# A position bias read in turned order through GpSimd's queue, and two later forget-bias operations, in a two-layer attention and feed-forward block

## The chip, the cores and the metric

The kernel runs on one core of one Trainium2 chip. The metric is the device time of one execution in microseconds (us); lower is better. The core has five engines with a queue each: PE (matmuls), DVE (elementwise and reductions on VectorE), ACT (ScalarE), POOL (GpSimd) and SP, which here only issues transfers. Each engine works through its own queue in order; semaphores tie the queues together. Transfers between DRAM and the on-chip memory are issued from a queue, too, and land some time after.

## The reference, cut to what matters

Two layers (DEPTH), each a mixer and a gated feed-forward part, for 256 tokens of width 1024, all in f32. The mixer has three kinds of heads: 4 FoX heads with a forget gate, 4 MoBA heads and 8 MLA heads. With 256 tokens and a MoBA block of 256 there is one block, so a MoBA head is causal attention with a T5 bias. The two things that this change touches are the forget bias and the T5 bias:

```python
def dense_causal_attention(q, k, v, log_decay_cum=None):
    ...
        s = jnp.einsum('bhqd,bhkd->bhqk', q_i, k).astype(jnp.float32) * scale
        if log_decay_cum is not None:
            s = s + blk[2][..., None] - log_decay_cum[:, :, None, :]
        qpos = t0 + jnp.arange(Q_BLOCK)
        s = jnp.where(kpos[None, :] <= qpos[:, None], s, -jnp.inf)
        p = jax.nn.softmax(s, axis=-1)
...
def moba_attention(q, k, v, t5_table):
    ...
        dist_own = qp[:, None] - (own * MOBA_BLOCK + offs)[None, :]
        s_own = (jnp.einsum('bhqd,bhkd->bhqk', q_i, k_own).astype(jnp.float32) * scale
                 + table_t[:, t5_bucket(dist_own)])
        s_own = jnp.where(dist_own >= 0, s_own, -jnp.inf)
...
def hybrid_mixer(h, w_in, b_forget, ...):
    ...
    log_f = jax.nn.log_sigmoid((f_logit + b_forget).astype(jnp.float32))
    F = jnp.cumsum(log_f, axis=1).transpose(0, 2, 1)
    o_f = dense_causal_attention(heads(q_f, FOX_HEADS), heads(k_f, FOX_HEADS), heads(v_f, FOX_HEADS), F)
    o_m = moba_attention(heads(q_m, MOBA_HEADS), heads(k_m, MOBA_HEADS), heads(v_m, MOBA_HEADS), t5_table)
```

The T5 bias depends on the distance of query and key and the head alone, and is the same in both layers.

## The kernel before, in words

Weights stream from DRAM through SP's queue. Each matmul weight is split into two float32r halves: ScalarE copies it to `wh` (L102), DVE subtracts for `wl` (L103), and PE makes three matmuls of each product (`mm3`, L146, and `mm3t`, L168). The raw weights have four buffers, the halves six each. A second stream, `adaw`, carries the weights of the modulation; four buffers hold it, and a chunk is either multiplied on PE (`adap`, L274) or reduced on DVE (L266, 128x1024).

Layer 0 begins with a warm-up of PE by 13 matmuls on a tile `zero` that GpSimd makes, then the sum of squares of `x` per token tile: ScalarE squares (L356), DVE adds, GpSimd takes the power (`rs`, L343), DVE makes a diagonal matrix `diag` of it (L361). Then `phase_a` (L578) goes through eight chunks of 128 rows; each multiplies a chunk of `adaw`, turns a chunk of `x` by the diagonals (`xT`, L949), modulates it on ScalarE (`hv`, L367), and adds its part to the products cq, ckv, qf and kf. In the last chunk the table `shp` is loaded. Then follow the norms, the value projections `vps`, the MLA pairs (`mla_pair`, L749), the FoX pairs and the MoBA pairs (`head_pair`, L769 on), between them further projections `qkp` and steps of the modulation (`fill`); then the output projection `y` and the feed-forward part, which makes up most of the time. Layer 1 repeats this with other stages at its start.

The T5 bias (`t5_bias`, L226) was computed behind the value projections of layer 0. A table `tab` and a one-hot matrix `oneh` are loaded; DVE repeats the table (`trep`), four matmuls give the band of 384 distances for each head on 32 partitions (`tp`, L235), ScalarE evicts it (`band`, L238), and four transfers write it to a DRAM tensor `scr`, so that it stands there 128 times per head (L242). One transfer then reads `mobab` from it, with each partition shifted by one element (L245). The MoBA softmax adds `mobab` (L433 and L435).

For the forget gate, `gqs` are the summed gates by token; `rows_of` (L299) transposes them, writes `row` to DRAM (`rowsgk`, L306) and reads it back onto all partitions (`gk`, L309). `fox_bias` (L725) makes `fb` of one head from `gk`, `gqs` and the mask in two operations of DVE: 128x128 (L729) and 128x256 (L732).

The order within each engine's queue comes from a scheduler that sorts by the program's order, by priorities and by its own estimates of time; `order_after` adds an order between two instructions without a wait. In `fox_bias` L729 was bound to come after the last maximum of a softmax so far (`last["max"]`, L435), L732 wasn't. Transfers on SP's queue are issued in that queue's order: a transfer that waits holds all behind it.

Of the kernel before, what the change touches and what calls it, by code (L numbers as in the profile page):

```python
# [8 lines left out]
F32 = mybir.dt.float32  # L9
# [4 lines left out]
P = 128  # L14
# [30 lines left out]
def block_kernel(ctx, tc, A, out):  # L45
# [141 lines left out]
    shp = const.tile([P, 896], F32, name="shp")  # L187
# [38 lines left out]
    def t5_bias():  # L226
        tab = wk.tile([P, 4], F32, tag="tab", bufs=1, name="tab")
        SP.dma_start(tab, A["t5"])
        oneh = wk.tile([P, 384], F32, tag="e", bufs=4, name="oneh")
        SP.dma_start(oneh, A["k_onehot"])  # L230
        trep = wk.tile([P, 4, 32], F32, tag="kt", bufs=2, name="trep")
        DVE.tensor_copy(trep, tab[:, :, None].to_broadcast([P, 4, 32]))
        tp = pg("tp")
        for hd in range(4):
            PE.matmul(tp[32 * hd:32 * hd + 32, :384], trep[:, hd, :], oneh, start=True, stop=True,  # L235
                      tile_position=(0, 32 * hd))
        band = wk.tile([P, 384], F32, tag="e", bufs=4, name="band")
        ACT.activation(band, tp[:, :384], AF.Copy)  # L238

        scr = dram.tile([4, 4, 32, 384], F32, name="scr")  # L240
        for q in range(4):
            SP.dma_start(scr[:, q, :, :], band)  # L242
        base = scr[:, :, :, :]
        toep = bass.AP(base.tensor, base.offset + 127, [[383, P], [P * 384, 4], [1, S]])
        SP.dma_start(mobab, toep)  # L245
# [276 lines left out]
    def mixer(l, h, prepare, fill, after):  # L522
# [168 lines left out]
        if l == 0:  # L691
            for i, ps in enumerate(rest):
                qk_out(ps, i)
            w1.extend(value_weights(l))
            for t in range(2):
                value1(t)
            t5_bias()
# [27 lines left out]
        def fox_bias(hd):  # L725
# [3 lines left out]
            i = DVE.scalar_tensor_tensor(fb[:, 0:P], gk[:, 0:P], gqs[:, 2 * hd:2 * hd + 1], mask[:, P:S],  # L729
                                         op0=ALU.subtract, op1=ALU.add)  # L730
            order_after(i, last["max"])
            DVE.scalar_tensor_tensor(fb[:, P:384], gk, gqs[:, 2 * hd + 1:2 * hd + 2], mask,  # L732
                                     op0=ALU.subtract, op1=ALU.add)
# [262 lines left out]
def _constants():  # L996
# [6 lines left out]
    out["k_ones"] = np.ones((P, P), f)  # L1003
    out["k_mask"] = np.where(j[None, :] <= P + p[:, None], 0.0, NEG).astype(f)
# [11 lines left out]
    oneh = np.zeros((P, 384), f)  # L1016
# [100 lines left out]
```

## Time and profile before

| | |
|---|---|
| median of 3 runs | 676.29 us (673.01 to 677.72) |
| the profiled execution | 677.55 us, of which the span from first to last instruction is 675.7 us |
| busy: PE, DVE, ACT, POOL | 638.3, 451.2, 365.7, 52.8 us |
| mean granted clock of TensorE | 0.986 of full |
| moved | 155.29 MB, mean 230 GB/s |

PE is busy for 94% of the span, so idle time of PE and stretches at the lower of its two clock levels are what there is to read; the slices of the page show where they are, the waits name who was waited for, and the chain of waits follows back what ended last. Times in rows are us from the span's start unless marked ns. In a chain row the first number is the start, the second the duration; in a timeline row the bracket at the end gives the idle time before and what ended it.

### The profile page before, as it was taken

The page shows a single profiled execution, that of the slowest core. Times are in us where ns is not written, and L with a number is a line of the kernel's source. Part 1 is how long each engine was busy: PE and PEld are TensorE (multiplying, and loading weights), DVE is VectorE, ACT ScalarE, POOL GpSimd, SP SyncE. Part 2 cuts the span into 40 slices and gives each one's busy share as a digit, 9 for nine tenths or more (in the row PEclk, how much of TensorE's full clock was granted, in tenths as well). Part 3 has the DMA queues.
Part 4 walks back from the last instruction along what each step waited for, and adds up shares of the span by engine and source line. Part 5 has one row for each costly group of instructions (what it writes and reads, how often), then busy time and mean ns, then how long its engine had stood idle before and what let it go on. Part 6 is the DMA issues. An engine that isn't in the chain of part 4 may idle for free.

```text
span 675.7 us, 12112 instructions
## 1 busy us (share of the span) xinstructions
PE 638.3 (94%) x4543; PEld 564.7 (84%) x4543; DVE 451.2 (67%) x969; ACT 365.7 (54%) x758; POOL 52.8 (8%) x90
## 2 busy tenths in 40 slices
PE   7988769999999999999998999899899999999996
PEld 5877658567999999999978988768799999999994
DVE  2557277878867777797658864875878755555543
ACT  4348436868644444443467764886764444444431
POOL 1000011431000000000001011250100000000000
PEclk8999979999999999999999999999999999999999
DMA  8968586786478898898845865651568676565511
GB/s 311 407 214 287 161 315 221 266 289 214 123 255 308 288 357 307 312 325 287 303 157 173 270 229 185 219 189 64 187 196 271 223 237 182 183 185 183 185 60 63
DMA packets 44410, 155.29 MB, mean 230 GB/s; under 512 B 5136, under 2 KB 6464, under 8 KB 44352
## 3 DMA queue, kind: packets, MB, share of 16 engines
q1 hardware_dynamic: 44352, 154.52, 67.7%
q8 instruction: 36, 0.59, 0.4%
q14 instruction: 22, 0.18, 0.1%
HBM read 152.64 MB, written 1.86 MB: 229 GB/s over the span
## 4 chain that ended last, share of the span: by engine, by line
PE 76%; DVE 8%; DMA 6%; ACT 3%; POOL 3%; issue 2%; SPq 0%; DVEq 0%; POOLq 0%; ACTq 0%
PE gu L148 11%; PE gu L149 11%; PE gu L150 11%; PE y L172 8%; PE y L170 8%; PE y L171 8%; DMA adaw<-in_w_ada_dram 4%; DVE wl L103 3%; PE adap L274 2%; PE o L478 2%; DMA scr<-band 2%; POOL rs L343 1%; PE qkp L150 1%; PE s L460 1%; PE qkp L148 1%
## 5 line engine op out<-in xcount | busy, mean ns | idle before, releaser
L103 DVE TENSOR_TENSOR wl<-raw_gu,wh 128x1024 fp32r<-128x1024 f32 (+1 forms) x100 | 108.5, 1095 | 67.8 <-ACT wh L102 66.8
L102 ACT ACTIVATE wh<-raw_gu 128x1024 fp32r<-128x1024 f32 (+1 forms) x100 | 94.2, 956 | 92.0 <-PE gu L149 62.5
L148 PE MATMUL gu<-h0fL,wh 128*128 128x256 f32 x304 | 86.2, 283 | 0.0
L148 PE MATMUL gu<-h1fL,wh 128*128 128x256 f32 x304 | 86.2, 283 | 0.0
L149 PE MATMUL gu<-h0fH,wh 128*128 128x256 f32 x304 | 86.0, 283 | 0.0
L149 PE MATMUL gu<-h1fH,wh 128*128 128x256 f32 x304 | 86.0, 283 | 0.0
L150 PE MATMUL gu<-h0fH,wl 128*128 128x256 f32 x304 | 86.0, 283 | 0.0
L150 PE MATMUL gu<-h1fH,wl 128*128 128x256 f32 x304 | 86.0, 283 | 0.0
L266 DVE CUSTOM_DVE_ANT_0 adaw<-adaw,crow 128x1024 f32<-128x1024 f32 x64 | 77.9, 1227 | 11.8 <-DMA adaw<-in_w_ada_dram 11.7
L102 ACT ACTIVATE wh<-raw_dn 128x1024 fp32r<-128x1024 f32 x44 | 46.6, 1060 | 54.8 <-issue 33.3
L171 PE MATMUL y<-wh,hid 128*128 128x512 f32 x176 | 69.6, 396 | 0.0
L170 PE MATMUL y<-wh,hid 128*128 128x512 f32 x176 | 69.5, 396 | 0.0
L172 PE MATMUL y<-wl,hid 128*128 128x512 f32 x176 | 69.5, 395 | 0.0
L103 DVE TENSOR_TENSOR wl<-raw_dn,wh 128x1024 fp32r<-128x1024 f32 x44 | 53.6, 1223 | 21.8 <-ACT wh L102 21.7
L149 PEld LDWEIGHTS gu<-h1fH,wh 128*128 128x128 f32 x304 | 58.3, 192 | 0.4
L149 PEld LDWEIGHTS gu<-h0fH,wh 128*128 128x128 f32 x304 | 58.3, 192 | 0.4
L148 PEld LDWEIGHTS gu<-h1fL,wh 128*128 128x128 f32 x304 | 58.2, 192 | 0.4
L148 PEld LDWEIGHTS gu<-h0fL,wh 128*128 128x128 f32 x304 | 58.2, 192 | 0.4
L150 PEld LDWEIGHTS gu<-h1fH,wl 128*128 128x128 f32 x304 | 58.3, 192 | 0.0
L150 PEld LDWEIGHTS gu<-h0fH,wl 128*128 128x128 f32 x304 | 58.3, 192 | 0.0
L343 POOL TENSOR_TENSOR rs<-rs,mhalf 128x1 f32<-128x1 f32 x16 | 11.0, 688 | 439.4 <-DVE rs L342 439.4
L172 PEld LDWEIGHTS y<-wl,hid 128*128 128x128 f32 x176 | 33.0, 188 | 8.0
(331 smaller groups left out, 1482.2 us busy)
## 6 DMA issues: line engine op xcount, KB each, us to landing
adaw<-in_w_ada_dram SPq DMA_DIRECT2D x96, 512.0 KB
raw_gu<-in_w_gu_dram SPq DMA_DIRECT2D x88, 512.0 KB
raw_dn<-in_w_dn_dram SPq DMA_DIRECT2D x44, 512.0 KB
raw_out<-in_w_out_dram SPq DMA_DIRECT2D x16, 512.0 KB
raw_b<-in_w_b_dram SPq DMA_DIRECT2D x12, 512.0 KB
raw_a<-in_w_a_dram SPq DMA_DIRECT2D x8, 448.0 KB
raw_uq<-in_w_uq_dram SPq DMA_DIRECT2D x4, 512.0 KB
raw_vm<-in_w_vm_dram SPq DMA_DIRECT2D x4, 512.0 KB
```

Of the source, the lines that this page charges most:

```text
L102: ACT.activation(dst_h, src, AF.Copy)
L103: return DVE.tensor_tensor(dst_l, src, dst_h.bitcast(F32), op=ALU.subtract)
L148: chain(PE.matmul(ps, w[0], x[1], start=start, stop=False))
L149: chain(PE.matmul(ps, w[0], x[0], start=False, stop=False))
L150: chain(PE.matmul(ps, w[1], x[0], start=False, stop=stop))
L170: PE.matmul(ps, x[1], w[0], start=start, stop=False)
L171: PE.matmul(ps, x[0], w[0], start=False, stop=False)
L172: PE.matmul(ps, x[0], w[1], start=False, stop=stop)
L266: i = DVE.tensor_tensor_reduce(out=raws[u], in0=raws[u], in1=crow, op0=ALU.mult, op1=ALU.add, scale=1.0, scalar=0.0, accum_out=sb[:, u:u + 1])
L274: chain(PE.matmul(ps[32 * g:32 * g + 32, :], crep[:, kc, :], raws[kc // 4][:, g * 256:(g + 1) * 256], start=kc < 4, stop=kc >= 4, tile_pos ...
L343: POOL.tensor_tensor(r, r, mhalf, op=ALU.pow)
L478: PE.matmul(o[64 * u:64 * u + 64, lo:lo + P], v[:, u * 64:(u + 1) * 64], ps[u][:, i * P:(i + 1) * P], start=start, stop=stop, tile_positio ...
```

## The change

It has two parts. The T5 bias is prepared at the very start: table and one-hot matrix have 64 rows instead of 128, one matmul makes the band on 4 partitions, one transfer writes the 6 KB of it to DRAM, and two transfers (two heads each) read from it rows that are shifted the other way round, so that partition p holds what partition 127-p needs; all of these are issued from GpSimd's queue. In the first layer two matmuls by a turned identity `flip`, a new part of `shp`, put the rows in their order, and ScalarE evicts them into `mobab`. In `fox_bias` both operations are now bound to come after the last maximum.

```diff
-    shp = const.tile([P, 896], F32, name="shp")
+    shp = const.tile([P, 1024], F32, name="shp")
+    flip = shp[:, 896:1024]
...
-    def t5_bias():
-        tab = wk.tile([P, 4], F32, tag="tab", bufs=1, name="tab")
-        SP.dma_start(tab, A["t5"])
-        oneh = wk.tile([P, 384], F32, tag="e", bufs=4, name="oneh")
-        SP.dma_start(oneh, A["k_onehot"])
-        trep = wk.tile([P, 4, 32], F32, tag="kt", bufs=2, name="trep")
-        DVE.tensor_copy(trep, tab[:, :, None].to_broadcast([P, 4, 32]))
+    def t5_load():
+
+        tab = wk.tile([64, 4], F32, tag="tab", bufs=1, name="tab")
+        POOL.dma_start(tab, A["t5"])
+        oneh = wk.tile([64, 384], F32, tag="e", bufs=4, name="oneh")
+        POOL.dma_start(oneh, A["k_onehot"])
         tp = pg("tp")
-        for hd in range(4):
-            PE.matmul(tp[32 * hd:32 * hd + 32, :384], trep[:, hd, :], oneh, start=True, stop=True,
-                      tile_position=(0, 32 * hd))
-        band = wk.tile([P, 384], F32, tag="e", bufs=4, name="band")
-        ACT.activation(band, tp[:, :384], AF.Copy)
-
-        scr = dram.tile([4, 4, 32, 384], F32, name="scr")
-        for q in range(4):
-            SP.dma_start(scr[:, q, :, :], band)
-        base = scr[:, :, :, :]
-        toep = bass.AP(base.tensor, base.offset + 127, [[383, P], [P * 384, 4], [1, S]])
-        SP.dma_start(mobab, toep)
+        PE.matmul(tp[0:4, :384], tab, oneh, start=True, stop=True)
+        band = wk.tile([4, 384], F32, tag="e", bufs=4, name="band")
+        ACT.activation(band, tp[0:4, :384], AF.Copy)
+        scr = dram.tile([4, 384], F32, name="scr")
+        POOL.dma_start(scr, band)
+        base = scr[:, :]
+        turned = [wk.tile([P, 512], F32, tag="yg", bufs=2, name="t5rows") for _ in range(2)]
+        for n in range(2):
+            POOL.dma_start(turned[n], bass.AP(base.tensor, base.offset + n * 768, [[1, P], [384, 2], [1, S]]))
+        return turned
+
+    def t5_bias(turned):
+        for n in range(2):
+            ps = pg("t5b")
+            PE.matmul(ps, flip, turned[n], start=True, stop=True)
+            ACT.activation(mobab[:, 2 * n:2 * n + 2, :], ps.rearrange("p (h j) -> p h j", h=2), AF.Copy)
+
+    t5 = t5_load()
...
-            i = DVE.scalar_tensor_tensor(fb[:, 0:P], gk[:, 0:P], gqs[:, 2 * hd:2 * hd + 1], mask[:, P:S],
-                                         op0=ALU.subtract, op1=ALU.add)
-            order_after(i, last["max"])
-            DVE.scalar_tensor_tensor(fb[:, P:384], gk, gqs[:, 2 * hd + 1:2 * hd + 2], mask,
-                                     op0=ALU.subtract, op1=ALU.add)
+            for t, sl, m in ((0, slice(0, P), mask[:, P:S]), (1, slice(P, 384), mask)):
+                i = DVE.scalar_tensor_tensor(fb[:, sl], gk[:, :sl.stop - sl.start],
+                                             gqs[:, 2 * hd + t:2 * hd + t + 1], m, op0=ALU.subtract, op1=ALU.add)
+                order_after(i, last["max"])
...
+    out["k_flip"] = np.eye(P, dtype=f)[::-1].copy()
...
-    oneh = np.zeros((P, 384), f)
+    oneh = np.zeros((64, 384), f)
```

The call of `t5_bias` stays behind the value projections in the program's order. The changed instructions stand in the queues as follows; the rows are line (of the kernel before or of the changed one), operation, tiles written and read, shape.

SP's queue from the weights `raw_b` of layer 0 on, first before, then changed:

```order
L126 DMA raw_b<-in_w_b_dram 128x1024 x4
L126 DMA raw_out<-in_w_out_dram 128x1024
L242 DMA scr<-band 4x32x384 x4
L306 DMA rowsgk<-row 8x128
L126 DMA raw_out<-in_w_out_dram 128x1024
L245 DMA mobab<-scr 128x4x256
L309 DMA gk<-rowsgk 128x1024
L257 DMA adaw<-in_w_ada_dram 128x1024 x3
L126 DMA raw_out<-in_w_out_dram 128x1024 x2
```

```order
L126 DMA raw_b<-in_w_b_dram 128x1024 x4
L126 DMA raw_out<-in_w_out_dram 128x1024
L263 DMA adaw<-in_w_ada_dram 128x1024
L312 DMA rowsgk<-row 8x128
L126 DMA raw_out<-in_w_out_dram 128x1024
L263 DMA adaw<-in_w_ada_dram 128x1024
L315 DMA gk<-rowsgk 128x1024
L126 DMA raw_out<-in_w_out_dram 128x1024
L263 DMA adaw<-in_w_ada_dram 128x1024 x2
L126 DMA raw_out<-in_w_out_dram 128x1024
```

The four writes of `scr` and the read of `mobab` are gone from between `raw_out` and `gk`, and `adaw` loads stand earlier.

DVE's queue from the reciprocals of the first MLA pair's softmax (`ri`) to the second pair's `qx`, `nm` and `ri`, first before, then changed (ISA is a reduction: of `adaw`, or of scores with a maximum):

```order
L443 RECIPROCAL ri<-sm 128x2 x2
L732 SCALAR_TENSOR_TENSOR fb<-gk,gqs,shp 128x256
L103 TENSOR_TENSOR wl<-raw_b,wh 128x1024
L763 TENSOR_TENSOR qx<-qp,qt 128x512
L266 ISA adaw,adasum<-adaw,crow 128x1024
L266 ISA adasum 128x1
L266 ISA adaw,adasum<-adaw,crow 128x1024
L266 ISA adasum 128x1
L320 TENSOR_TENSOR gcol<-adasum,first 128x2
L433 ISA e,mx<-s,shp 128x128
```

```order
L272 ISA adaw,adasum<-adaw,crow 128x1024
L272 ISA adasum 128x1
L449 RECIPROCAL ri<-sm 128x2 x2
L326 TENSOR_TENSOR gcol<-adasum,first 128x2
L327 TENSOR_TENSOR gcol<-gcol,first 128x2
L103 TENSOR_TENSOR wl<-raw_b,wh 128x1024
L768 TENSOR_TENSOR qx<-qp,qt 128x512
L272 ISA adaw,adasum<-adaw,crow 128x1024
L272 ISA adasum 128x1
L439 ISA e,mx<-s,shp 128x128
L439 ISA mx 128x1
```

The `fb` that needs `gk` no longer stands ahead of the split of raw_b and of `qx`; one `adaw` reduction moved ahead of the reciprocals.

POOL's queue at the start, from the small constants on, first before, then changed (`rs` is the power for one of the two token tiles):

```order
L192 MEMSET mhalf 128x1
L194 MEMSET zf 128x128
L198 MEMSET epsc 128x1
L196 CAST zero<-zf 128x128
L343 ISA
L343 TENSOR_TENSOR rs_132<-rs_132,mhalf 128x1
L343 TENSOR_TENSOR rs_142<-rs_142,mhalf 128x1
```

```order
L193 MEMSET mhalf 128x1
L195 MEMSET zf 128x128
L199 MEMSET epsc 128x1
L230 DMA tab<-in_t_dram 64x4
L197 CAST zero<-zf 128x128
L232 DMA oneh<-in_k_onehot_dram 64x384
L349 ISA
L349 TENSOR_TENSOR rs_146<-rs_146,mhalf 128x1
L238 DMA scr<-band 4x384
L349 TENSOR_TENSOR rs_156<-rs_156,mhalf 128x1
L242 DMA t5rows<-scr 128x2x256 x2
```

Two loads stand among the constants, and the write of `scr`, which waits for `band`, stands between the powers of the two token tiles.

## Rows read from the trace of the kernel before

**Rows 1.** The page's part 2: busy tenths of PE and granted clock by slice

```profile
PE   7988769999999999999998999899899999999996
...
PEclk8999979999999999999999999999999999999999
```

**Rows 2.** PE's waits, 0 to 135 us: total us, times, longest

```profile
PE s L458 <- DVE qx L763: 8.1, 2, 7.2
...
PE pt L451 <- POOL e L445: 1.7, 2, 1.2
```

**Rows 3.** DVE's waits, 40 to 135 us

```profile
DVE fb L732 <- DMA gk<-rowsgk: 8.3, 1, 8.3
```

**Rows 4.** The chain of waits, 58 to 112 us

```profile
69.29 10.34 DMA scr<-band
...
80.12 5.44 DMA gk<-rowsgk
...
85.99 1.22 DVE wl L103
...
87.86 1.22 PE s L458 x4
...
90.79 1.47 PE o L478 x10
...
92.78 0.21 PE qkp L148
...
94.18 0.12 PE qkp L149
...
103.97 5.04 DMA adaw<-in_w_ada_dram
```

**Rows 5.** The timeline of SP's queue, 62 to 112 us

```profile
67.42 3.10 SPq L242 DMA_DIRECT2D scr<-band  x4
71.03 0.86 SPq L306 DMA_DIRECT2D rowsgk<-row  x1
```

**Rows 6.** The timeline of all engines, 74 to 114 us

```profile
76.91 0.48 POOL L445 TENSOR_SCALAR e<-e,ri 128x256 f32<-128x256 f32 x1
...
77.52 1.06 ACT L102 ACTIVATE wh<-raw_b 128x1024 fp32r<-128x1024 f32 x1 [0.39 <-ACT e L441]
```

**Rows 7.** The instructions on the tile tp: ns min/median/max, first and last start

```profile
L235 PE MATMUL tp<-oneh,trep x8: 486/498/510, 65.9 to 66.2; 128*32 128x384 f32 x8
L238 ACT ACTIVATE band<-tp x1: 491/491/491, 66.9 to 66.9; 128x384 f32<-128x384 f32 x1
```

**Rows 8.** The timeline of all engines, 0 to 13 us

```profile
6.21 1.95 PE L220 MATMUL crow<-first,cr 128*128 128x128 f32 x16
...
10.00 0.64 PE L274 MATMUL adap<-adaw,crep 128*32 128x256 f32 x8 [1.84 <-DMA adaw<-in_w_ada_dram]
...
10.37 0.58 ACT L221 ACTIVATE crow<-crow 128x512 f32<-128x512 f32 x1
...
10.79 0.55 POOL L343 TENSOR_TENSOR rs<-rs,mhalf 128x1 f32<-128x1 f32 x1 [2.37 <-DVE rs L342]
...
11.38 0.29 DVE L361 TENSOR_SCALAR diag<-first,rs 128x128 f32<-128x128 f32 x1 [0.47 <-POOL rs L343]
...
11.76 1.01 PE L949 MATMUL xT<-diag,x 128*128 128x128 f32 x4
```

**Rows 9.** The instructions on the tile scr

```profile
L242 SPq DMA_DIRECT2D scr<-band x4: 522/602/1233, 67.4 to 69.3; - x4
```

**Rows 10.** The timeline of all engines, 43 to 75 us

```profile
47.48 0.36 PE L148 MATMUL cq<-h0aL,wh 128*128 128x256 f32 x1 [1.69 <-ACT wh L102]
...
50.49 0.39 ACT L669 ACTIVATE acq<-cq 128x256 f32<-128x256 f32 x1 [1.71 <-PE cq L619]
```

**Rows 11.** The timeline of all engines, 98.5 to 99.9 us

```profile
98.67 1.22 DVE L266 CUSTOM_DVE_ANT_0 adaw<-adaw,crow 128x1024 f32<-128x1024 f32 x1
98.68 1.56 POOL L445 TENSOR_SCALAR e<-e,ri 128x256 f32<-128x256 f32 x1
```

More of the change, by code (lines that the diff above doesn't have):

```diff
@@ L696, in mixer @@
                 value1(t)
-            t5_bias()
+            t5_bias(t5)
         kx = act.tile([P, 8, S], F32, tag="kx", name="kx")
@@ L1015, in _constants @@
     dist = 255 - np.arange(384)
-    oneh = np.zeros((P, 384), f)
+    oneh = np.zeros((64, 384), f)
     oneh[np.where(dist >= 0, _bucket(dist), 32), np.arange(384)] = 1.0
     out["k_onehot"] = oneh
-    shapes = np.concatenate([out.pop(k) for k in ("k_tri", "k_ones", "k_ktab", "k_mask", "k_qtab")], axis=1)
+    shapes = np.concatenate([out.pop(k) for k in ("k_tri", "k_ones", "k_ktab", "k_mask", "k_qtab", "k_flip")], axis=1)
     out["shapes"] = shapes
@@ L1028, in _layout @@
     o["x"] = g["x"][0].reshape(2, P, D).transpose(1, 0, 2)
-    o["t5"] = np.concatenate([g["t5_table"], np.full((1, 4), NEG, np.float32), np.zeros((P - 33, 4), np.float32)])
+    o["t5"] = np.concatenate([g["t5_table"], np.full((1, 4), NEG, np.float32), np.zeros((64 - 33, 4), np.float32)])
     o["b_forget"] = g["b_forget"]
```

## The prediction

> **What bounds the kernel now.** First read the slices of the page: PE is at nine tenths or more nearly everywhere, except in the first slices and in the two between 68 and 101 us, where it falls to 7 and 6 and the granted clock to 9 and 7 tenths [rows 1]. So a gain must come from those holes. Next, PE's waits in the first 135 us: the largest by far is the score matmuls of the second MLA pair, which wait for `qx` on DVE, 7.2 us at a stroke [rows 2]. DVE's own waits say why `qx` is late: DVE stood 8.3 us in front of one `fb` for the transfer of `gk` [rows 3]. DVE works in order, so the split of the last raw_b unit and `qx`, which need no `gk`, stood behind it. The chain of waits tells why `gk` came so late: the four copies of the band to DRAM, issued from 67.42 us, take until 79.6; the read of `mobab` waits for them on SP's queue, the read of `gk` is behind that, and lands at 85.56 [rows 4, 5]. Its source, `rowsgk`, had been issued at 71.03. After the hole PE starts at 87.86 us on the low clock: in the chain a `qkp` matmul costs 0.21 us at 92.78 and 0.12 at 94.18, the 1.2 and the 2.4 GHz level [rows 4].
>
> **Part 1, SP's queue and the later `fb`.** Both changes cut the same wait, so they are one term. The five T5 transfers leave SP between `raw_out` and `gk`, so `gk` can be issued as soon as `rowsgk` has landed, at about 72 to 73 us, and lands before 80 even at the 5.44 us it takes now. And `fb`, bound to come after the last maximum issued so far, no longer stands ahead of `qx`. What is late next for `qx` is the split: ScalarE makes `wh` of that raw_b from 77.52 for 1.06 us, so DVE can start at 78.6. From the start of that split to the scores now takes 87.86 - 85.99 = 1.87 us, so the scores start at 80.5 instead of 87.86: 7.4 us gained [rows 4, 6]. If DVE loses a stretch of this (the order puts one `adaw` reduction of 1.2 us ahead of the two reciprocals, but that ends before 78.6), it is lost one for one; bounds -7.4 and -5.
>
> **Part 2, the clock.** The scores and the ten `o` matmuls ran on the low level from 87.86 to 92.26 us (90.79 + 1.47), 4.4 us in the chain; at the other level half of it, 2.2, is saved. From 92.26 to 94.06 `qkp` ran at 0.21 in place of 0.12, which is 0.8 more. With PE idle for about one us instead of seven I take the full 3.0; bounds -3.0 and 0 [rows 4].
>
> **Part 3, work removed near 66 us.** The four band matmuls (eight records, the last from 66.2 to 66.7 us) leave PE, and the band's 0.49 us leaves ScalarE. PE is nearly full there, but DVE ends some of its waits soon after, so I take half: -0.4, bounds -0.8 and 0 [rows 7].
>
> **Part 4, the start.** What the change adds runs early. On GpSimd's queue two loads stand ahead of and behind the cast of `zero`, which the warm matmuls wait for; a microsecond there moves the `crow` matmuls from 8.16 us to 9.2 at most, and PE's next work waits for `adaw` until 10.00 anyway [rows 8], so the warm part is free. The `tp` matmul (64 rows by 384 columns, two records of 0.5 us at most by the old ones) goes in the same hole. The new wait is elsewhere: the copy `scr<-band` is on GpSimd ahead of the second `pow` of the row norms. The band is evicted behind the second `crow` (starts 10.37, 0.58 us), so it ends near 11.4; then comes the DMA instruction, which no row here shows on GpSimd; the nearest are SP's issues of `scr<-band`, 0.52, 0.60 (median) and 1.23 us [rows 9], and I take 0.6; then `pow` 0.55 and the diagonal 0.29. The second half of `xT` so starts at 12.9 or so, against 12.27 now (11.76 plus half of 1.01) [rows 8]. Queued behind `pow` is nothing on GpSimd but the two row reads; but behind `xT` stands all of PE, and PE has no wait in the eight chunks that follow but the first two of `adaw`, so the shift of 0.6 us goes to the end of that stage: +0.6, bounds 0.3 and 1.3.
>
> The Trainium skill speaks against this place: "DMA: Bandwidth & Descriptors", section "Latency and other measured facts", gives a first byte of about 1 us for a DMA issued from GpSimd and 0.6 from the sync or scalar path. By its 1 us the term would be an estimated +1.0 and the sum 0.4 smaller; no run here shows it.
>
> **Part 5, the bias itself.** Two f32 matmuls of 512 columns stand before the last chunk of the first stage, where PE waits 1.69 us now for ScalarE and DVE [rows 10]. Scaling the old records (0.498 us for 384 columns) they take 1.3 us if their two passes overlap and 2.7 if not; the second needs a PSUM buffer that the last `hv` frees. I take +0.2, bounds 0 and 1.0. The two evictions of some 0.6 us each on ScalarE lie before a stretch in which it waits for PE's last `cq` matmul, 1.71 us before `acq` [rows 10]; the value weights come later by the first of them, which that idle time covers. `flip` rides in the shapes load, which is issued early. The moved `fb` costs DVE 0.48 us later, beside the wait of the old order: nothing.
>
> **Part 6, what is late next.** After the scores the second pair's softmax shares DVE with `adaw` reductions, as now, and GpSimd's scaling of `e` suffers beside them: 0.48 us alone, 1.56 beside a reduction that starts at the same moment (98.67 us) [rows 6, 11]. PE's `pt` waits for those 1.7 us in two pieces now [rows 2]. In the new order all six `pt` precede the scores of the third pair, so PE waits for all four scalings: one more slow scaling, 1.1 us, and some low clock behind it. I take +1.5, bounds 0 and 4.3 (four slow ones). The feed-forward part keeps PE full and only starts earlier.
>
> **Sum.** -7.4 - 3.0 - 0.4 + 0.6 + 0.2 + 1.5 = -8.5 us. The profiled execution took 677.55 us (span 675.7 and 1.85 around it), so it would be 669.05. It lies 1.26 us above the median of the runs shown, 676.29; taken from that, the forecast is 667.8 us.
>
> **Rivals.** (a) The wait changes its name: DVE's order now has reductions of `adaw` among the maxima of the second pair, each of which waits for a transfer, and a DVE that stands there stands before the softmax. For it: SP's queue issues these loads in order behind `gk`, and a wait for `adaw` of 5.04 us is in the chain at 103.97 [rows 4]. Against: SP's queue is no longer held until 79.6, so those loads go out from 72 us on, and the buffers they need are free. One such wait costs 5.0: -8.5 + 5.0 = -3.5, or 672.8 us.
> (b) The idle time moves to `pt`, waiting for GpSimd, and the clock falls there instead. For it: [rows 11]. Against: the largest `pt` wait now is 1.2 us [rows 2]. Part 2 is lost: -5.5, or 670.8 us.
> (c) Slower: the bias matmuls, which stand in PE's order before the last chunk of the first stage, wait for the row reads on GpSimd's queue. If that queue is served only when SP's stream leaves room, the rows come after it. Every us after 45.8 us (the start of the wait in [rows 10]) is paid by the whole kernel, so from 8.5 us after that, 54.3 us, the kernel is slower; at 58 us it would be some +3.7, or 680 us. Against: the rows can be asked for by about 14 us, and they are only 512 KB, the size of `gk`, which took 5.44 us [rows 4].
>
> The Trainium skill has a rule that would lead there: "SBUF — State Buffer", section "SBUF: two separate sides", says that while DVE runs an operation that takes the port it shares with GpSimd, GpSimd can't write the descriptors of its DMAs. [rows 11] agree that DVE slows GpSimd; how long its DMAs suffer no run here shows.
>
> **How the numbers follow.** Forecast 0.70, (a) 0.15, (b) 0.11, (c) 0.04. The forecast's own bounds: best -7.4 - 3.0 - 0.8 + 0.3 = -10.9 (665.4 us), and worst -5 + 0 + 0 + 1.3 + 1.0 + 4.3 = +1.6, which needs all bad ends together; with the four largest halfway it is about -2 (674). Cases (a) and (b) lie inside; a little more at the low end for stages in which the earlier loads help: 663.0 to 675.5 us. About 1% is what a measurement of this kernel tells from no change: 669.5 us. Of the forecast some eight tenths lie below that (0.56), of (b) a third; with (a) nearly all within: faster 0.60, same 0.36, slower 0.04.
>
> **What would show it.** Right: no wait of DVE for `gk`; the scores of the second pair at about 80 to 82 us; a granted clock that stays full from 80 to 94 us; the second diagonal at 12.6 us and the first stage's end 0.6 to 1 us later than now. Wrong: `xT` after 14 us, the bias matmuls waiting for a DMA, DVE waiting for `adaw` before the second softmax, or `pt` waiting more than 3 us for GpSimd.

## The result, and the profile after

The changed kernel takes 670.07 us (median of 5 runs, 668.2 to 670.45), the kernel before beside it 676.30 (5 runs, 673.01 to 677.72): the ratio is 0.9909, with a 95% interval of 0.9885 to 0.9933. The forecast was 667.8 us in a range of 663.0 to 675.5. So the gain is 6.2 us where 8.5 were forecast. The interval leaves no doubt that it is a gain, but at 0.9% it falls short of the 1% that the prediction took as the border: by its own measure this is the outcome "same", to which it gave 0.36, and not "faster", to which it gave 0.60.

The profiled execution took 670.45 us (span 668.7), that of before 677.55 (675.7). First the slices of the page, against [rows 1]:

```profile
PE   7998889899999999999999999899999999999996
...
PEclk9999989999999999999999999999999999999999
```

The hole between 68 and 101 us, 7 and 6 tenths of PE before, is filled to 8 and 8, and the clock in it is 9 and 8 tenths where it was 9 and 7. PE's waits up to 135 us (total, times, longest) answer to [rows 2]:

```profile
PE pt L457 <- POOL e L451: 3.1, 3, 1.1
...
PE pt L457 <- POOL e L450: 1.8, 1, 1.8
...
PE s L464 <- DVE qx L768: 0.9, 1, 0.9
```

The 7.2 us of the scores for `qx` are gone, and what is late now is `pt`, which waits 4.9 us in four pieces for GpSimd's scaling of `e` (2.8 before, 1.7 of it in [rows 2]). On DVE the wait of `fb` for `gk`, 8.3 us in [rows 3], isn't there any more; the largest wait for a transfer is this (four of them, the longest 2.8):

```profile
DVE adaw L272 <- DMA adaw<-in_w_ada_dram: 4.7, 4, 2.8
```

The chain of waits shows the same stretch from inside, against [rows 4] (start, us, what):

```profile
67.53 4.94 DMA rowsgk<-row
72.49 0.33 SPq L315
...
73.35 4.00 DMA adaw<-in_w_ada_dram
77.35 0.35 POOL e L450
77.70 1.43 POOL e L451
...
80.22 0.64 PE s L464 x4
...
86.54 2.26 POOL e L450
...
90.28 1.49 PE pt L457 x5
```

SP issues the read of `gk` at 72.49 instead of 80.12 and the next `adaw` at 73.35. The second pair's scores start at 80.22 in this view (80.15 in the timeline of PE) in place of 87.86. The piece that names `adaw` up to 77.35 is no wait of DVE: what ended there was GpSimd's scaling before (see part 1 below). Then GpSimd sets the pace: at 86.54 a scaling that takes 0.35 us elsewhere takes 2.26, and PE waits for it.

To see where the time went over the whole span, I read the start of eight steps from the timelines of PE and from the instructions on the feed-forward tiles (us; the last kernel is the changed one again, profiled a second time, in a run of 667.23 us):

| step | before | after | after, 2nd profile |
|---|---|---|---|
| first `cq` of the first chunk | 16.59 | 16.13 | 16.34 |
| first `vps` | 51.96 | 51.82 | 52.05 |
| scores of MLA pair 1 | 73.14 | 71.47 | 71.67 |
| scores of MLA pair 2 | 87.86 | 80.15 | 80.53 |
| first FoX scores, layer 0 | 119.03 | 108.05 | 107.66 |
| first `gu`, layer 0 | 185.5 | 176.0 | 173.9 |
| first FoX scores, layer 1 | 434.94 | 424.88 | 422.61 |
| first `gu`, layer 1 | 498.1 | 491.1 | 487.8 |
| span | 675.7 | 668.7 | 665.3 |

The change is 11.0 us ahead at the FoX scores of layer 0, 10.1 at those of layer 1, and 7.0 at the end. So it gains more than was forecast and gives some back, and the largest piece that it gives back lies between the last two steps of layer 1: 63.2 us before, 66.3 after. There one wait of PE stands that before doesn't have, and behind it the clock falls (stretch, PE's busy time and the others', then the granted clock, the share of the DMA engines and GB/s):

```profile
PE st L424 <- DVE acc L490: 2.1, 1, 2.1
```

```profile
431.50:434.60 3.10, 1.01 (x10) 0.52 (x8) 3.10 (x17) 2.82 (x13) 2.17 (x3) 0.99 0.12 48
434.60:437.00 2.40, 2.38 (x14) 1.09 (x18) 2.10 (x7) 1.77 (x7) 2.40 (x4) 0.50 0.62 218
```

### The profile page after: what moved, and what is told of

Its sections match the earlier page's. It is cut to its first block, busy times and chain, and to the rows that moved or that the text cites. A ratio compares the mean times of both kernels' runs of the same rounds, so it can differ in the third digit from the quotient of the medians.

```text
span 668.7 us, 12104 instructions
## 1 busy us (share of the span) xinstructions
PE 639.3 (96%) x4541; PEld 564.3 (84%) x4541; DVE 452.0 (68%) x968; ACT 367.3 (55%) x760; POOL 58.6 (9%) x95
## 4 chain that ended last, share of the span: by engine, by line
PE 79%; DVE 7%; DMA 4%; ACT 3%; POOL 3%; issue 2%; DVEq 0%; SPq 0%; POOLq 0%; ACTq 0%
PE gu L148 11%; PE gu L149 11%; PE gu L150 11%; PE y L170 7%; PE y L172 7%; PE y L171 7%; DMA adaw<-in_w_ada_dram 2%; DVE wl L103 2%; PE adap L280 2%; PE o L484 2%; PE pt L457 1%; PE qkp L148 1%; PE qkp L150 1%; PE qkp L149 1%; PE s L466 1%
```

## The experiments

Two questions: which half of the change brings the gain, and where do the 3 us in layer 1 come from? The first guess on the second was the later `fb`, which the change binds in both layers. Each experiment was profiled once; medians and ratios to the kernel before on the same chip follow.

**One half at a time.** `e1_fb_only` is the kernel before with the new `fox_bias`; `e2_t5_only` is the changed kernel with the old one, by this edit:

```diff
-            for t, sl, m in ((0, slice(0, P), mask[:, P:S]), (1, slice(P, 384), mask)):
-                i = DVE.scalar_tensor_tensor(fb[:, sl], ...)
-                order_after(i, last["max"])
+            i = DVE.scalar_tensor_tensor(fb[:, 0:P], ...)
+            order_after(i, last["max"])
+            DVE.scalar_tensor_tensor(fb[:, P:384], ...)
```

Expected of the first:

> The kernel before with only the two forget-bias operations bound to come later; the T5 bias still goes through SP's queue. Theory (the stall was DVE standing in order before fb): the second pair's scores start at 80.5 to 82 us though gk still lands at about 85; feed-forward part of layer 0 begins 7 to 9 us earlier than before (first gu at 176.5 to 178.5 instead of 185.5); layer 1 loses about 3 us as in the changed kernel, so 669.5 to 672.5 us. Rival (SP's queue, held until 79.6 us, costs by itself, as adaw and raw_out come late): DVE waits for adaw instead and the scores or the second softmax stay late; gain in layer 0 under 5 us, 674 us or more.

Measured: 674.73 us (10 runs), ratio 0.9971 [0.9952, 0.9989]. The wait of DVE in front of the softmax stays and changes its name; on PE it moved from the second pair's scores to the third's `qp`:

```profile
DVE adaw L266 <- DMA adaw<-in_w_ada_dram: 8.5, 1, 8.5
```

```profile
PE qp L148 <- DVE mx L435: 7.2, 1, 7.2
```

SP's queue still issues `gk` at 79.85 and `adaw` at 80.36 there. The second pair's scores start at 79.47, but the third's at 96.01, against 91.56 in the changed kernel. So the later `fb` alone moves the wait by one pair; rival (a) of the prediction is what this half does, and its wait is 8.5 us where the rival had 5.0.

> The changed kernel without the later forget bias (the 128x256 one is unbound, as before). Theory: gk is asked for at about 72 us and lands near 78, so DVE waits for it one us or so and the scores start at 80 to 82 us; layer 1 keeps the order of the kernel before and does not lose its 3 us: 666.5 to 668.5 us. Rival (without the binding the wait for gk stays 3 us or more): scores at 83 us or later and 669.5 us or more.

Measured: 667.92 us (664.32 to 671.03, 4 runs), ratio 0.9862 [0.9810, 0.9915]; profiled at 664.32. No wait of DVE for `gk` over 1.0 us, second pair at 80.87, third at 91.76. The T5 half alone does what the whole change does, and is not slower than it.

**The later `fb` in layer 0 alone.** `e3_fb_l0` is the changed kernel with one condition:

```diff
-                order_after(i, last["max"])
+                if t == 0 or l == 0:
+                    order_after(i, last["max"])
```

> The changed kernel with the new binding of the forget bias in layer 0 only; layer 0 has the changed kernel's order on PE and DVE, layer 1 that of the kernel before. Theory (the changed kernel loses 2.5 to 3 us in layer 1 because the new order puts an adaw reduction ahead of acc, for which PE's st waits 2.1 us, and the clock falls behind it): first gu of layer 1 at about 488 us instead of 491.1, the whole 2.5 to 3 us faster than the changed kernel, 667 to 667.8 us. Rival (the loss comes with the earlier start of layer 1, from transfers that arrive no earlier): 669.5 to 670.5 us, as the changed kernel.

Measured: 666.34 us (664.37 to 668.67, 4 runs), ratio 0.9852 [0.9816, 0.9888]. The wait of `st` for `acc` is gone, and layer 1 takes 63.2 us from its FoX scores to its first `gu`, as before.

**Later transfers on GpSimd's queue.** `e4_scr_late` moves the copy `scr<-band` and the two row reads behind the second `pow` of the row norms:

```diff
+        return band
+
+    def t5_rows(band):
         scr = dram.tile([4, 384], F32, name="scr")
         POOL.dma_start(scr, band)
...
+            t5 = t5_rows(t5b)
```

> The changed kernel with the write of scr behind the second power of the row norms on GpSimd; all else in the same order. Theory: the second diagonal at 11.5 us instead of 12.76, xT no longer waits 0.95 us, the first chunk is then bound by wh at 13.0, so the first cq matmul of chunk 0 comes at about 15.6 instead of 16.13: 0.5 us faster than the changed kernel, 669.5 us. Rival (with the wait gone or moved, PE falls to the low clock between 12 and 15 us as in the kernel before): the first cq matmul at 16.1 us or later, no gain.

Measured: 671.57 us (4 runs), ratio 0.9919 [0.9894, 0.9945]: no gain over the changed kernel. `adac` of the first chunk comes at 12.91 instead of 13.42, but the first `cq` at 16.50 instead of 16.13. The timeline of PE says what was late next:

```profile
11.77 0.64 PE L283 MATMUL adap<-adaw,crep 128*32 128x256 f32 x8 [0.56 <-DMA adaw<-in_w_ada_dram]
...
13.87 0.50 PE L614 MATMUL cq<-wh,zero 128*128 128x512 f32 x1 [0.52 <-ACT wh L102]
```

The half microsecond is taken up by the second half of `adaw` and by `wh`.

**What holds `st` in layer 1.** In the changed kernel's order a reduction of `adaw` stands ahead of `acc` on DVE (432.79, 1.24 us; `acc` at 434.04). `e5_acc_first` ties this one column's reductions behind `acc`:

```diff
                 if last.get("ffn"):
                     order_after(i, last["wl"])
+                elif l == 1 and which == 1 and j == 7:
+                    order_after(i, last["acc"])
...
-                DVE.tensor_tensor(self.acc, self.acc, sq, op=ALU.add)
+                last["acc"] = DVE.tensor_tensor(self.acc, self.acc, sq, op=ALU.add)
```

> The changed kernel with one more tie: in layer 1, the two DVE reductions of the last adaw column are ordered behind the sum acc of the MLA group's squares; the later fb stays. My theory: the later fb in layer 1 pushed the first of these reductions (1.24 us) ahead of acc, and PE's st stood 2.1 us for acc. Then the wait of st for acc falls below 1 us and the stretch from layer 1's first FoX score to its first up-projection, 66.2 us in the changed kernel and 63.2 in the kernel before, falls to 64.5 or less; time about 668, a microsecond or two under the changed kernel. Rival: it is the place of the four MoBA maxima and of the fb themselves that costs, and the wait only changes its name: the stretch stays at 65 to 66.5.

Measured: 671.05 us (663.6 to 673.76, 9 runs), ratio 0.9894 [0.9857, 0.9931]. My theory fell: `acc` stands ahead of the reduction, and `st` waits as long as it did. The timelines of DVE and ScalarE show why:

```profile
435.43 0.47 DVE L492 TENSOR_TENSOR acc<-acc,osq 128x256 f32<-128x256 f32 x1 [0.65 <-ACT osq L490]
```

```profile
433.45 0.40 ACT L448 ACTIVATE e<-e,nm 128x128 f32<-128x128 f32 x1 [0.28 <-DVE nm L446]
...
434.35 0.36 ACT L488 ACTIVATE oc<-o 128x256 f32<-128x256 f32 x1
434.61 0.39 ACT L448 ACTIVATE e<-e,nm 128x128 f32<-128x128 f32 x1
...
434.99 0.40 ACT L490 ACTIVATE osq<-oc 128x256 f32<-128x256 f32 x1
```

PE was done with `o` at 432.46 there, but ScalarE took the exponentials of one more softmax ahead of `oc`, and one between `oc` and `osq`. With the later `fb` in layer 0 alone the same two lines read, in the second profile of that kernel (`e6_fb_l0_again`), where `o` ends at 433.05:

```profile
433.10 0.38 ACT L486 ACTIVATE oc<-o 128x256 f32<-128x256 f32 x1
...
433.90 0.41 ACT L488 ACTIVATE osq<-oc 128x256 f32<-128x256 f32 x1
```

`oc` comes at once. In the changed kernel itself `osq` ends at 433.88 and the reduction on DVE at 434.03: both hold `acc`, within 0.2 us of each other.

**Chance or order?** The next two run the kernel with the later `fb` in layer 0 alone and the changed kernel once more, on one chip.

> The changed kernel with the later fb in layer 0 alone, again, beside the changed kernel itself on the same chip. If the later fb in layer 1 costs 2 to 3 us, this is faster than the changed kernel by 2 to 4 us (0.3 to 0.6%) and the layer 1 stretch is again 63.3 us. Rival: its lead of 3.7 us in the first look was one of stretches on the low clock that come and go, and the medians lie within 1.5 us.

> The changed kernel once more, nothing edited. Its layer 0 is the same code as that of the one with the later fb in layer 0 alone, yet that one reached layer 0's first FoX score 2.7 us sooner, on a full clock between its MLA pairs. If that was chance, this run shows a first FoX score anywhere between 105 and 108.5 us; if the same low stretch comes again at 90 to 94 us, it hangs on something that layer 1 can't change, which would be hard to explain. The layer 1 stretch must be 66 us again if its cause is the order.

Measured: 667.57 us (666.24 to 671.28, 6 runs), ratio 0.9878 [0.9851, 0.9905], and 670.57 us (666.09 to 676.13, 10 runs), ratio 0.9918 [0.9887, 0.9949]. By the ratios they are 2.7 us apart (3.7 between the medians of the first runs); the intervals still overlap. Of the traces, the stretch of layer 1 is 63.2 and 65.2 us. The lead in layer 0 didn't come again: this time the FoX scores came at 107.11 with the edit and at 107.66 without. Most of it goes with the time at which one `adaw` transfer landed. In the first two profiles DVE stood 2.77 us (changed kernel) and 0.86 us (`e3_fb_l0`) for it, ahead of the second pair's maxima:

```profile
82.14 1.23 DVE L272 CUSTOM_DVE_ANT_0 adaw<-adaw,crow 128x1024 f32<-128x1024 f32 x1 [2.77 <-DMA adaw<-in_w_ada_dram]
```

```profile
80.02 1.23 DVE L272 CUSTOM_DVE_ANT_0 adaw<-adaw,crow 128x1024 f32<-128x1024 f32 x1 [0.86 <-DMA adaw<-in_w_ada_dram]
```

In all eleven profiles with T5 on GpSimd's queue this wait is there, 0.8 to 3.1 us long, and the third pair's scores start 9.4 to 11.1 us after that reduction starts: between the first two profiles the reduction differs by 2.1 us and the scores by 1.9, and in the profiles of this pair of runs (80.99 with the edit, 80.95 without) they differ by 0.04 and 0.1. The other 0.8 of the 2.7 us lie behind the third pair's scores, where the clock differs. The windows of 88 to 96 us in the first profiles of the changed kernel and of `e3_fb_l0`, in this order:

```profile
88.00:92.00 4.00, 2.05 (x9) 1.53 (x10) 3.00 (x7) 1.82 (x6) 3.03 (x4) 0.73 0.72 238
92.00:96.00 4.00, 4.00 (x31) 3.30 (x31) 1.61 (x11) 1.87 (x9) 0.00 (x0) 0.85 0.54 173
```

```profile
88.00:92.00 4.00, 2.91 (x24) 2.16 (x24) 2.54 (x13) 1.39 (x4) 1.36 (x2) 1.00 0.82 275
92.00:96.00 4.00, 4.00 (x42) 3.34 (x40) 1.19 (x6) 3.50 (x11) 1.90 (x4) 1.00 0.77 248
```

The code is the same up to there. In these windows PE pauses for 2.0 and 1.1 us, and the clock falls in one and not in the other.

**Size or queue?** `e8_t5_sp` keeps the small copy, but issues all T5 transfers from SP's queue at the old place, and the bias matmuls before the fifth pair:

```diff
-        POOL.dma_start(scr, band)
+        SP.dma_start(scr, band)
...
-            t5_bias(t5)
+            t5.append(t5_load())
...
             if i == 4:
                 o = new_h(f"o{l}")
+                if l == 0:
+                    t5_bias(t5[0])
```

> The small T5 copy on SP's queue at the old place: loads, one copy of 4x384, and the two row reads are issued by SP between raw_vm and rowsgk as the large ones were; the bias matmuls and evictions move to the fifth pair. The later fb stays. It tells the size of the copy from the queue it is on. If the size is what counts, SP is free at 72 us, DVE waits nowhere over 3 us and the time is that of the changed kernel, 668 to 671. If the queue counts, the row reads wait on SP for the small copy to land (4 to 6 us as for rowsgk now), rowsgk and gk are behind them, gk lands after 83 us and adaw after that: DVE waits 3 to 6 us for adaw in front of the second or third pair, and the time is 671 to 675.

Measured: 673.68 us (672.51 to 677.29, 10 runs), ratio 0.9969 [0.9950, 0.9988]. The time is in the span of the second theory, the mechanism is that of the first. SP's queue:

```profile
60.34 0.33 SPq L238 DMA_DIRECT2D scr<-band  x1
...
61.69 0.90 SPq L242 DMA_DIRECT2D t5rows<-scr  x2
...
70.44 0.33 SPq L314 DMA_DIRECT2D gk<-rowsgk  x1
```

`gk` goes out at 70.44, the list of DVE's waits from 66 to 112 us has none for a transfer, and the second and third pair start at 81.24 and 91.26, like the changed kernel. So the small size alone frees SP's queue. But the fourth pair starts at 107.28 (102.42 in the changed kernel) and `pt` waits 6.9 us in all for GpSimd up to 135 us (4.9 there). What in the new order makes the third pair that long wasn't tried; the 3 us between this kernel and the changed one on the same chip are open.

**Both ties.** `e9_osq_first` puts the exponentials of the second unit of the last FoX pair behind `osq` on ScalarE; `e10_osq_acc_first` has this and the tie of `e5_acc_first`:

```diff
-        ACT.activation(e[:, 0:P], e[:, 0:P], AF.Exp, bias=nm[:, 0:1], accum_out=sm[:, 0:1])
+        last["unit"] = ACT.activation(e[:, 0:P], e[:, 0:P], AF.Exp, bias=nm[:, 0:1], accum_out=sm[:, 0:1])
...
-            ACT.activation(sq, self.oT[:, j, :], AF.Square)
+            i = ACT.activation(sq, self.oT[:, j, :], AF.Square)
+            if self.l == 1 and self.n == 512 and j == 3:
+                order_after(last["unit"], i)
```

> The changed kernel with one tie on ScalarE instead: in layer 1 the exponentials of the second unit of the last FoX pair come behind osq of the MLA group, so that oc and osq stand one softmax earlier. With acc ahead of adaw on DVE, st still waited 1.9 us, and DVE's wait named osq. New theory: st is held by two things that end within 0.2 us of each other, osq on ScalarE and the adaw reduction on DVE. Then this tie alone does nothing: acc now waits out the reduction, st waits 1.5 us or more, and the layer 1 stretch stays at 65 us. Rival: osq alone held it, and the reduction would have been done in time: st waits under 1 us, stretch 64 or less.

Measured: 669.59 us (4 runs), ratio 0.9882 [0.9828, 0.9935]. Neither: `st` doesn't wait, but the stretch is 67.0 us. The wait moved to `pt` (0.8 us for ScalarE, 0.7 for GpSimd), and behind it the clock was 0.57 of full from 435 to 440 us:

```profile
PE pt L457 <- ACT pts L459: 0.8, 1, 0.8
...
```

> Both ties, acc ahead of the reduction and osq ahead of the exponentials, with the later fb in both layers. If the two together are what the later fb cost in layer 1, the wait of st falls below 1 us, the layer 1 stretch from 65.2 to 64 or less, and the time is that of the kernel with the later fb in layer 0 alone (666 to 668). Rival: the loss lies in the order of the whole stretch, and something else is late next (pt for the exponentials that were pushed back): the stretch stays above 64.5.

Measured: 669.12 us (665.51 to 672.32, 6 runs), ratio 0.9888 [0.9851, 0.9925]. `st` doesn't wait, the clock stays full, and the stretch is 64.2 us: one of the two microseconds is back, the other now stands as `pt` for GpSimd (0.8) and `adac` for ScalarE (0.5):

```profile
PE pt L459 <- POOL e L453: 0.8, 1, 0.8
...
PE adac L294 <- ACT adasb L285: 0.5, 1, 0.5
```

So neither instruction alone is what stands wrong. Binding `fb` in layer 1 changes the order of the FoX and MoBA softmaxes on DVE and ScalarE together, and two ties don't put it back.

**Is the later `fb` worth anything?** The T5 half alone, beside the version with the later `fb` in layer 0, on one chip.

> The T5 part alone, the order of fb as before in both layers, beside the next kernel. With SP's queue free gk lands by 80 us or sooner, so DVE has no long wait in front of fb to be spared: I expect the same time as with the later fb in layer 0 alone, 667 to 668.5, no wait of DVE for gk over 1 us, and a layer 1 stretch of 63.2 us. Rival: the later fb in layer 0 still saves a wait of 1 to 2 us, and this one is slower by that much.

> The later fb in layer 0 alone, for the comparison on one chip with the T5 part alone: 666 to 668, layer 1 stretch 63.2 us. If the later fb is worth something once the T5 transfers are off SP's queue, it is faster than the T5 part alone by 1 us or more.

Measured: 668.26 us (667.07 to 669.13, 4 runs), ratio 0.9880 [0.9864, 0.9895], and 668.88 us (665.04 to 671.25, 6 runs), ratio 0.9885 [0.9859, 0.9911]. No difference: once the T5 transfers are off SP's queue the later `fb` in layer 0 brings nothing that can be measured. The layer 1 stretch is 63.2 us in both.

The stretch of layer 1 in all profiles, from its first FoX scores to its first `gu`, and the clock in it, is the cleanest result of the study:

| `fb` in layer 1 | kernels on full clock from 425 to 450 us | with a fall of the clock there |
|---|---|---|
| old place | before 63.2, e2 63.1, e3 63.2, e6 63.2, e11 63.2, e12 63.2 | none |
| later | e1 65.4, e4 65.2, e7 65.2, e8 65.2 | changed kernel 66.3, e5 65.2 |
| later, with osq tied | e10 64.2 | e9 67.0 |

On full clock the later `fb` costs 2.0 to 2.2 us in layer 1, with or without the T5 half. Taken without it there, the T5 change is a better kernel than the one measured: 666.3 to 668.9 us in five sets of runs, ratios of 0.985 to 0.9885, against 670.07 and 670.57 us, 0.9909 and 0.9918. The intervals of single sets overlap; it is the stretch that makes it sure.

## Why the prediction was right, and where it was not

The terms against the steps of the profiled pair (us; the difference of each stretch, after less before):

| stretch | predicted | measured |
|---|---|---|
| start to first `vps` (parts 4, 5) | +0.8 | -0.1 |
| to pair 1 (part 3) | -0.4 | -1.5 |
| pair 1 to pair 2 (part 1) | -7.4 | -6.0 |
| pair 2 to FoX, layer 0 (parts 2, 6) | -1.5 | -3.3 |
| FoX to `gu`, layer 0 | 0 | +1.5 |
| `gu` to FoX, layer 1 | 0 | -0.6 |
| FoX to `gu`, layer 1 | 0 | +3.1 |
| rest | 0 | 0.0 |
| sum | -8.5 | -7.0 |

Of the prediction's signs of being right three came: no wait of DVE for `gk`, the scores at 80.15 us, the second diagonal at 12.76. The clock that stays full from 80 to 94 us and the later end of the first stage didn't. Two of its signs of being wrong came as well: DVE waits 2.77 us for `adaw` before the second softmax, and `pt` waits 4.9 us for GpSimd, where 3 was the limit. So the time lies in the range and the cause of the gain was right, but what is late next was worse than taken and a loss in layer 1 wasn't in the sum; the median of 670.07 is nearer to the 670.8 of rival (b) than to the forecast.

**Part 1 named the right cause; that its time fits is in part luck.** The scores of the second pair were to start at 80.5 us and start at 80.15, but the stretch itself fell by 6.0 and not by 7.4 us; the steps before it, which came out 2.0 us better than forecast, made that good. The issue of `gk` at 72.49, where 72 to 73 was said, is another such meeting: the working left 1 to 2 us from the issue of `rowsgk` at 71.03 to its landing, while `rowsgk` is now issued at 67.53 and takes 4.94. It was the queue, as the argument said: `e2_t5_only` has them at 80.87 without the later `fb`. That "both changes cut the same wait, so they are one term" was right for the sum and too kind to the later `fb`: alone it renames the wait and brings 2 us. What is late at 80.15 isn't the split, though. `qx` is done at 79.37; the scores stand on PE behind `pt`, which waits for a scaling on GpSimd that takes 1.44 us beside the split, 0.48 alone:

```profile
77.51 1.27 DVE L103 TENSOR_TENSOR wl<-raw_b,wh 128x1024 fp32r<-128x1024 f32 x1 [0.43 <-ACT wh L102]
77.68 1.44 POOL L451 TENSOR_SCALAR e<-e,ri 128x256 f32<-128x256 f32 x1
78.69 0.68 DVE L768 TENSOR_TENSOR qx<-qp,qt 128x512 f32<-128x512 f32 x1
79.17 0.44 PE L457 MATMUL pt<-first,e 128*128 128x128 f32 x2 [1.08 <-POOL e L451]
```

Rival (a) comes one step later and in a small form, in the row of 82.14 above: behind `qx` DVE stands 2.77 us for `adaw`, ahead of the second pair's maxima. The load had been issued at 73.35, as early as the prediction argued against the rival, but landed 8.8 us later. The second pair's softmax and PE's wait for `pt` come behind it (parts 2 and 6).

**Part 3 was too small.** The band's eight matmul records cost PE 0.85 us of busy time before; half was taken, since DVE ended some of the waits. The stretch fell by 1.5 us, as it does in all profiles with T5 moved to GpSimd (19.4 to 20.0 us, against 21.2 before and in `e1_fb_only`). What gave more than the matmuls' own time wasn't tried apart and stays open.

**Part 4 had the delay right and the sign wrong.** The tasks came as worked out: GpSimd's DMA instruction took 0.58 us (0.6 taken), and the second diagonal starts at 12.76 (12.6), `xT` at 13.10 (12.9). The timeline of 9 to 17 us:

```profile
11.54 0.58 POOL L238 DMA_DIRECT2D scr<-band  x1 [3.57 <-ACT band L236]
...
12.76 0.29 DVE L367 TENSOR_SCALAR diag<-first,rs 128x128 f32<-128x128 f32 x1 [1.97 <-POOL rs L349]
13.10 0.49 PE L954 MATMUL xT<-diag,x 128*128 128x128 f32 x2 [0.95 <-DVE diag L367]
...
13.56 0.47 PE L611 MATMUL cq<-wh,zero 128*128 128x512 f32 x1
...
16.57 0.80 POOL L242 DMA_DIRECT2D t5rows<-scr  x1 [3.85 <-DMA scr<-band]
```

But the kernel before ran its profile of this place on the low level: the granted clock was 0.50 from 12 to 15 us, its `cq` on `zero` took 0.80 us where the row here has 0.47. The view by slices shows no more of that than an 8 in its first place ([rows 1]); the window does:

```profile
12.00:15.00 3.00, 2.89 (x13) 1.74 (x16) 1.70 (x5) 1.80 (x3) 0.00 (x0) 0.50 1.03 416
```

`e1_fb_only` and `e8_t5_sp`, which have the old start and ran it on a full clock, reach `cq` at 15.45 and 15.16; ten of the eleven profiles with the new start reach it at 15.84 to 16.71, the other (`e9_osq_first`) at 15.12. So the new start has a price, mostly 0.4 to 1.5 us, and it was hidden by what the profile of before lost on the low clock. How much of it is the write ahead of the power isn't shown: `e4_scr_late`, without that write there, comes at 16.50. Nor was the way right by which the term was to reach the end of the stage: PE was said to have no wait in the chunks but the first two of `adaw`, and [rows 10] have one of 1.69 us before the last.

The Trainium skill, "DMA: Bandwidth & Descriptors", section "Latency and other measured facts", would have made this term an estimated 1.0 by its first byte of 1 us. The part that the wait depended on was the instruction's own 0.58 us; the first byte can't be seen here, only the landing (below).

**Part 5 held for the bias.** The four records of the bias matmuls take 2.1 us in the gap before the last chunk, which starts 30.8 us after the first one as it did before (30.9). The transfers had landed long before, so rival (c) didn't come: the rows were issued at 16.57 and 17.4 us, PE took them at 45.19 with no wait. The bill came one step later, at `vps`, 4.88 us after the start of that chunk instead of 4.48, as in the other profiles with the bias matmuls there; 0.4 in all, for the 0.2 taken.

**Parts 2 and 6 both came, and the rest lies where no part looked.** From 80 to 87 us the clock is full, and the scores with the ten `o` take 2.3 us (80.15 to 82.45) in place of 4.4: that is part 2. But PE then stands 2.84 us for `pt` (2.34 before), and the clock falls behind it, 0.73 and 0.85 of full from 88 to 96 us, as rival (b) has it. From pair 2 to pair 3 the gain is 1.3 us, close to the 1.5 of both parts together. The other 2.0 us lie between pair 3 and FoX. The piece of 5.04 us for `adaw` at 103.97 in [rows 4] isn't what was saved there: PE was busy from 104 to 110 us in the kernel before, and stood only 0.53 us, for `pt`, from pair 3 to FoX. These 0.53 are gone; three `pt` matmuls, some 0.4 us, now stand ahead of pair 3; the rest, 1.1 us by an estimate from the difference, goes to the clock, which was 0.54 in the first window, of the kernel before, and is 0.75 in the second, of the changed one:

```profile
100.50:104.00 3.50, 3.50 (x15) 3.04 (x14) 2.81 (x12) 0.67 (x2) 1.50 (x2) 0.54 0.69 239
104.00:110.00 6.00, 6.00 (x55) 5.61 (x55) 4.54 (x13) 4.38 (x10) 0.83 (x2) 0.98 0.40 142
```

```profile
91.50:95.00 3.50, 3.50 (x25) 2.80 (x24) 1.30 (x10) 1.06 (x3) 0.00 (x0) 0.75 0.50 164
```

That part 6 was a real price shows in the row of 86.54: GpSimd's 0.35 us became 2.26. It starts beside an `adaw` reduction of DVE (86.30, 1.20 us) and ends 0.15 us after the split behind it (87.43, 1.22 us). "SBUF — State Buffer" of the Trainium skill, section "SBUF: two separate sides", says that whoever of the two has the shared port keeps it for the whole instruction; the row agrees, and shows that a scaling can stand through two instructions of DVE, where [rows 11] had one.

**The step that failed** is a sentence of part 5: "The moved `fb` costs DVE 0.48 us later, beside the wait of the old order: nothing." It looked at layer 0 alone, where there was a wait to hide it. `fox_bias` runs in layer 1, too, where DVE waits for no `gk`, and there the later `fb` took the softmaxes out of their order, at 2.0 us on full clock, and 1.1 more in this profile, in which the clock fell behind the wait. The sum also put the stretch from FoX to `gu` in layer 0 at nothing, without a row for it. (That "the feed-forward part keeps PE full and only starts earlier" held: from `gu` to FoX of layer 1 and after the last `gu` the difference is -0.6 and 0.0.) It got longer by 1.5 us here, and by -0.2 to +3.8 in the other profiles with T5 on GpSimd's queue, with `pt` waiting for GpSimd and a clock of 0.66 from 130 to 140 us in the two that lost most (`e4_scr_late` and `e6_fb_l0_again`). `e2_t5_only` and `e11_t5_only_again`, without the later `fb`, have -0.2 and +1.6, so it comes without the later `fb`, too; whether the later `fb` adds to it, and what causes it, wasn't tried. The windows of 130 to 140 us, of the changed kernel and of `e6_fb_l0_again`:

```profile
130.00:140.00 10.00, 9.17 (x48) 6.54 (x48) 6.33 (x17) 4.70 (x11) 0.78 (x1) 0.83 0.71 224
```

```profile
130.00:140.00 10.00, 8.91 (x43) 5.94 (x43) 4.26 (x13) 4.43 (x11) 1.10 (x1) 0.66 0.63 217
```

With the 2.0 us in layer 1 in the sum, the forecast would have been 669.8 us, 0.3 us from the median. That closeness is luck: the other stretches of the table miss by 2.9 us one way and by 4.4 the other.

## What to carry to other kernels

Where a change binds an instruction later to spare it a wait, count every place where that line of code runs: bind it only where the wait is. Where a blocked queue is freed, the loads behind it go out earlier, but ask of each when it lands: here one landed 8.8 us after its issue, and DVE stood 2.8 us for it. A transfer in the chain of waits isn't yet idle time of the engine that bounds the kernel: beside the 5.04 us for `adaw` PE was busy, so read its own waits in that stretch. And before a small term is taken from a timeline, read the granted clock of that very stretch: the profile of one execution may hold a low stretch that the next hasn't.

## What was not expected of the hardware

**The clock falls or doesn't, in the same program at the same place.** A pause of 2.1 us before `st` in layer 1 is followed by a clock of 0.50 in the first profile of the changed kernel and by full clock in the second (`e7_after_again`):

```profile
432.30:434.70 2.40, 2.20 (x22) 1.04 (x22) 2.33 (x8) 2.21 (x9) 2.40 (x4) 1.00 0.67 224
```

In layer 0 the pauses around 90 us cost the clock in eight of the eleven profiles with T5 on GpSimd's queue, and not in `e2_t5_only`, `e3_fb_l0` and `e9_osq_first`; PE stood 2.76 us from pair 2 to pair 3 in the first of these and kept its clock, and 1.90 in `e7_after_again` and lost it. The times spread, too: `e5_acc_first` from 663.6 to 673.8 us in 9 runs, the kernel before from 674.4 to 679.0 in 24 runs on the same chip. That the clock behind short pauses is what spreads them is likely, but with one profile of each it isn't shown. With 4 runs of each a difference of 2 us can't be seen in the medians; it was the stretch in the traces that showed it.

**Small transfers land late beside the stream of weights, from either queue.** The issues of the changed kernel (KB each, median us from issue to landing), then two of `e8_t5_sp`:

```profile
t5rows<-scr POOLq DMA_DIRECT2D x2, 256.0 KB, 7.4
...
tab<-in_t_dram POOLq DMA_DIRECT2D x1, 1.0 KB, 5.3
```

```profile
t5rows<-scr SPq DMA_DIRECT2D x2, 256.0 KB, 6.1
...
tab<-in_t_dram SPq DMA_DIRECT2D x1, 1.0 KB, 5.2
```

From GpSimd's queue 1 KB takes 5.3 us and 256 KB 7.4; from SP's, at another place in the kernel, the same two take 5.2 and 6.1. What differs more is the issue: each holds GpSimd for 0.54 to 0.80 us, where SP issued the same row reads in 0.39 and 0.46. The whole chain of load, matmul, copy and read back runs from the first load at 1.33 us to the last rows, issued at 17.4 and landed at about 25: some 24 us in this kernel, waits for other work among them.
